# Spacing the transposes of finished attention heads behind the last projection slab, and a home in freed buffers for two output weights

## The chip, the cores and the metric

The kernel runs on one NeuronCore of a Trainium2 chip. The metric is the device time of one execution in microseconds (us), as the median of several. The core has five engines that run beside each other, each through its own list of instructions in order: TensorE (PE in the profile: matrix products and transposes, with PEld for the loading of its stationary operand), VectorE (DVE), ScalarE (ACT), GpSimd (POOL), and SyncE (SP), whose queue here only starts DMA transfers. PE writes its results to PSUM, a small memory of eight banks; the other operands live in SBUF.

## The reference

The model is a trunk of two layers over 512 tokens of width 1024. The first layer holds a causal convolution module, the second differential attention; each is followed by a gated feed-forward block (SwiGLU) and by a gated per-layer embedding. All is float32. The change touches the end of the second layer's attention. For each of eight heads `h`, with two sets of queries and keys of 64 channels, and values of 128 channels:

```python
qkv = x @ w_qkv                       # x is rms-normed before
q, k = rms_norm(q), rms_norm(k)       # per head and set
logits = q @ k.T + bias, causal       # two sets c = 0, 1
w = softmax(logits[0]) - lam * softmax(logits[1])
o = rms_norm(w @ v) * sub_g * (1 - lambda_init)
h = h + concat(o over heads) @ w_o    # 1024 x 1024
```

Then comes `h = h + swiglu(rms_norm(h))`, and then `h = h + sigmoid(rms_norm(h) @ w_gate) * (p @ w_proj)`, where `p @ w_proj` does not depend on `h`.

## The kernel before

Activations are held transposed: channels on the 128 partitions in eight chunks, tokens along the row. To keep float32 precision, every large product is made of three matmuls (`mm3`, lines 165 to 167): each operand is split into a high part `hi`, rounded to a shorter format, and a remainder `lo`, and the kernel sums lo·hi, hi·lo and hi·hi. So each weight tile of 128 x 1024 takes a load by SP into `wraw` (two buffers, line 154), a cast on ACT into `whi` (line 158) and a subtraction on VectorE into `wlo` (line 160). `whi` and `wlo` are rings of four buffers each; a new weight's cast waits until PE has done with the weight four places before it. Activations are split in the same way by `split_scaled` (lines 179 and 180: ACT, then VectorE).

The order of the instructions on each engine is not the order of the source. The program is built with a planner (`schedule_with_timeline_sim=True`): it plays the program through with its own estimates of durations, lets each engine take the earliest instruction in source order that is ready by that estimate, and writes the order down. The chip then runs each engine's list in that fixed order, with semaphore waits. Buffers of a tag go to the next tile of that tag when all readers of an earlier one are done.

The attention is made of 32 blocks, eight heads by four blocks of 128 queries. Each passes four stages:

- `stage_s` (line 953): scores on PE into an `sc` bank (two banks), bias and row extreme on VectorE (line 972), exponential on ACT (976), the combination of both sets on VectorE (979 to 981).
- `stage_t` (984): transposes on PE into a `tp` bank (two banks, line 989), evacuated by ACT (991).
- `stage_a` (997): product with the values on PE (1003) into the head's `mm` bank (four banks), evacuated by ACT (1008). With the fourth block of a head come its norm factors (1011 to 1020) and the scaling on POOL (1022).
- `stage_o` (1026), once per head: four transposes on PE into a `tp` bank (1029), then the split by ACT and VectorE (179, 180) into the tiles `A0` to `A15`, which are the operands of the output product.

The list `stages` (1037 to 1041) holds the first three stages in a software pipeline: block count `n` runs from 0 to 34, and a count issues the scores of block `n`, the transposes of block `n - 2` and the value product of block `n - 3`. While the projection slabs of queries, keys and values are multiplied (1047 to 1061), 63 of these 96 stages are issued between their matmuls. Behind the last slab 33 are left, from `n` = 22 on, and `step()` (1066) issues them one at a time: three steps beside each of the eight feature projections `p @ w_proj` (`project`, 1077 to 1083, two products each; their two weights are called projection weights below), and then one step after each product of the output projection (`linear`, called in 1095, with `heads_until` ahead of each product so that its head is there). After its stage, `step()` looks whether heads are finished: a head counts as finished when `(n - LA - 3) // 4` exceeds its number, with `LA = 3`; when no stages are left, `n` is set to 99.

`linear` (571) makes eight output chunks `m` of eight products `k` each (`k` is the head). Chunks 0 and 1 are made together, the others one by one. Each takes a weight from the ring and sums in an `mm` bank. `add_attn` (1091) adds a chunk to `h` and prepares the norm and operands of the feed-forward block. Behind it, lines 1096 to 1103 copy the first four feature projections to other tiles by DMA, and the feed-forward block begins; its first operands are normed into tiles of the tags C2, C3, C4 and split into C0, C1 and C5 (lines 618 to 625).

The tags C0 to C5 (two buffers each) hold the queries and keys of a pair of heads during the attention: C0 and C1 the queries, C2 to C5 the keys and their remainders. Two pairs are there at a time.

Of the kernel before, what the change touches and what calls it, by code (L numbers as in the profile page):

```python
# [13 lines left out]
F32R = mybir.dt.float32r  # L14
# [6 lines left out]
P = 128  # L21
S = 512
D = 1024
NC = D // P
NH = 8
# [49 lines left out]
LA = 3  # L75
# [17 lines left out]
def trunk(ctx, tc, xT, pT, wts, diag, dww, vec, rel, onehot, lamv, out):  # L93
    nc = tc.nc
    V, A, G, T = nc.vector, nc.scalar, nc.gpsimd, nc.tensor
# [7 lines left out]
    def sb(shape, tag, bufs, dt=F32):  # L103
        uid[0] += 1
        return pool.tile(shape, dt, tag=tag, name=f"{tag}_{uid[0]}", bufs=bufs)

    def ps(tag, bufs, shape=(P, S)):
        uid[0] += 1
        return psum.tile(list(shape), F32, tag=tag, name=f"{tag}_{uid[0]}", bufs=bufs)

    mm = lambda: ps("mm", 4)
    sc = lambda: ps("sc", 2)
# [20 lines left out]
    t = wk()[:, 0:P]  # L133
# [4 lines left out]
    t = tp()  # L138
# [4 lines left out]
    wnext = [0]  # L143
    loaded = [None]

    def weight(n=1024, pieces=1, between=(), eng=V, after=None, behind=None):
        i = wnext[0]
        wnext[0] += 1
        raw = sb([P, 1024], "wraw", 2)
        hi = sb([P, 1024], "whi", 4, F32R)  # L150
        lo = sb([P, 1024], "wlo", 4, F32R)
        for k in range(pieces):
            cut = slice(k * n // pieces, (k + 1) * n // pieces)
            loaded[0] = nc.sync.dma_start(raw[:, cut], wts[i, :, cut])
            if k < len(between):
                between[k]()
            with tc.issue_after(behind.ins) if behind else nullcontext():
                A.copy(hi[:, cut], raw[:, cut])  # L158
            with tc.issue_after(after.ins) if after else nullcontext():
                eng.tensor_tensor(lo[:, cut], raw[:, cut], f(hi[:, cut]), ALU.subtract)  # L160
        return hi, lo

    def mm3(acc, a, b, first, last):
        (ah, al), (bh, bl) = a, b
        T.matmul(acc, al, bh, start=first, stop=False)  # L165
        T.matmul(acc, ah, bl, start=False, stop=False)  # L166
        return T.matmul(acc, ah, bh, start=False, stop=last)  # L167

    def wpart(w, k):
        return tuple(t[:, k * P : (k + 1) * P] for t in w)  # L170
# [71 lines left out]
    def load(c):  # L242
        return lambda: nc.sync.dma_start(h[c], xT[c])

    w0 = weight(pieces=2, between=(load(0),))
    norm.operands(0)
    w1 = weight(pieces=2, between=(load(1), load(2)))
    pair_loads = [loaded[0]]
    pairs = [(w1, w0)]
# [4 lines left out]
    for c in range(1, NC):  # L254
        norm.operands(c)
    pairs.append((weight(), weight())[::-1])
    pair_loads.append(loaded[0])
    for c in range(NC):
# [19 lines left out]
    def project(ph, m, w, o, step=lambda: None):  # L278

        acc = mm()  # L280
        for k in range(2):
            last_product[0] = mm3(acc, wpart(w, 2 * (m % 4) + k), ph[k], k == 0, k == 1)
            step()
        A.copy(o, acc)
        return o
# [4 lines left out]
    accs = {}  # L290
# [275 lines left out]
            if c >= 1:  # L566
                z_lo.append(V.tensor_tensor(z[c - 1][1], y[c - 1], f(z[c - 1][0]), ALU.subtract))

    def linear(n_in, src, consume, group0=1, before=None, after=None, first=(None,) * 3, then=(None, None)):


        m = 0
        while m < NC:
            g = group0 if m == 0 else 1
            if m == group0:
                ws = [weight(n_in * P, behind=then[0], after=then[1])]
            else:
                ws = [weight(n_in * P, after=first[i] if m == 0 else None) for i in range(g)]
            accs = [mm() for _ in range(g)]
            for k in range(n_in):  # L580
                if before:
                    before(k)
                for w_, a_ in zip(ws, accs):
                    mm3(a_, wpart(w_, k), src[k], k == 0, k == n_in - 1)
                    if after:
                        after()
            for i in range(g):
                consume(m + i, accs[i])
            m += g
# [3 lines left out]
    def add_conv(m, acc):  # L593
        V.scalar_tensor_tensor(h[m], acc, col("b_pw2", m), h[m], ALU.add, ALU.add)
        norm.chunk(m)

    linear(NC, z, add_conv, 3, first=(None, last_sum[0], shifted), then=(z_hi[5], z_lo[5]))


    def ffn(norm, after, space):  # L600
# [133 lines left out]
        for at, (f0, n) in enumerate(PARTS):  # L734
            hid = []
            for pair in range(n // 2):
# [3 lines left out]
                if (at, pair) in SEVEN:  # L740
                    while making:
                        feed()
                    i = wnext[0]
                    wnext[0] += 4
                    gs = strassen(i)
                    for t in gs:
                        A.activation(t, t, AF.Silu)
                    us = strassen(i + 1)
                    for o, (t, g) in enumerate(zip(us, gs)):
                        V.tensor_tensor(t, t, g, ALU.mult)  # L750
                        first, step = (H2, H2) if o else (0, S + H2)
                        hs, ls = (bass.AP(x.tensor, x.offset + first, [list(x.ap[0]), [step, 2], [1, H2]]) for x in (hi, lo))
                        A.copy(hs, t.rearrange("p (a s) -> p a s", a=2))
                        V.tensor_tensor(ls, t.rearrange("p (a s) -> p a s", a=2), f(hs), ALU.subtract)
                    continue
# [30 lines left out]
            def add(m, acc):  # L786
                V.tensor_tensor(h[m], acc, h[m], ALU.add)  # L787
                if at == len(PARTS) - 1:
                    after.chunk(m)

            linear(n, hid, add, 2)

    def ple(norm, pp, after, last_cuts=1):
# [41 lines left out]
    for k in range(2):  # L835
        t = tp()
# [27 lines left out]
    def slab(n, cols):  # L864
        per = 1024 // cols
        ws = [weight(eng=G if i < n else V) for i in range(NC // per)]
        return [tuple(t[:, j * cols : (j + 1) * cols] for t in w) for w in ws for j in range(per)]
# [156 lines left out]
    ot = {}  # L1024

    def stage_o(hd):
        t = tp()
        for i in range(4):
            T.transpose(t[:, i * P : (i + 1) * P], osb[hd][:, i * P : (i + 1) * P], ident)
        hi = sb([P, S], f"A{2 * hd}", 1, F32R)  # L1030
        lo = sb([P, S], f"A{2 * hd + 1}", 1, F32R)
        split_scaled(t, gains[:, 1:2], hi, lo)
        ot[hd] = (hi, lo)
# [9 lines left out]
    def take(n):  # L1043
        got, stages[:n] = [s for _, s in stages[:n]], []
        return got

    waiting = None
    for what, at, pace in QKV:
        ws = slab(GLO if what == "q" and at > 0 else 0, P * at[1] if what == "v" else S)
        for tb in range(4):  # L1050
            if (what, at, tb) == ("v", (6, 2), 0):
                ph = pfeatures(1, [both(sb([P, 2, S], t, 1, F32R)) for t in ("B0", "B1")])
            between = take(3 * pace[tb])
# [7 lines left out]
                waiting = unit(at, ws, tb, between)  # L1061


    done = [0]

    def step():
        if stages:
            n, s = stages.pop(0)
            s()
        else:  # L1070
            n = 99
        while done[0] < NH and (n - LA - 3) // 4 > done[0]:
            stage_o(done[0])
            done[0] += 1

    pp = []
    for m in range(NC):
        if m % 4 == 0:
            w = weight()
        step()  # L1080
        if m % 2 == 0:
            o2 = sb([P, 2, S], f"B{m // 2 + 2}", 1) if m < 4 else sb([P, 2, S], f"C{m // 2 + 1}", 2)
        pp.append(project(ph, m, w, o2[:, m % 2], step))
# [7 lines left out]
    def add_attn(m, acc):  # L1091
        V.tensor_tensor(h[m], acc, h[m], ALU.add)
        norm.chunk(m)

    linear(NC, ot, add_attn, 2, heads_until, step)
    for m in (0, 1):
        o = sb([P, S], f"D{m + 2}", 1)
        nc.sync.dma_start(o, pp[m])
# [140 lines left out]
```

## Time and profile before

| | us |
|---|---|
| median of three runs (lowest to highest) | 1248.58 (1246.25 to 1249.45) |
| the profiled execution, whole | 1246.33 |
| its span, first to last instruction | 1244.6 |
| PE busy | 1232.6 (99%) |
| VectorE busy | 879.7 (71%) |
| ScalarE busy | 613.9 (49%) |
| GpSimd busy | 266.3 (21%) |

The granted clock of PE is 0.997 over the span. Times in the views count from the start of the span. A row of the timeline has the start, the length, the engine, the line of the kernel, the operation, the tiles written and read, shapes, and a count; a bracket at its end is the idle time of the engine before it and the work that ended it. In views of waits stand the total, the times and the longest. Matmuls overlap: on PE the distance from start to start is the cost, and not the length. The last slab's products end at 763.4 us, and the last product of the output projection stands near 844 us.

### The profile page before, as it was taken

Reading aid. Unit: us, or ns where it says so; the run is one execution under the profiler, and the core shown is the slowest. Engines: PE = TensorE matmul, PEld = TensorE weight load, DVE = VectorE, ACT = ScalarE, POOL = GpSimd, SP = SyncE. Lnnn points to the kernel's source line nnn. Section 1 sums busy time; section 2 is a strip of 40 time slices with the busy share of each in tenths; the row PEclk is TensorE's granted clock in tenths of the full one; section 3 lists DMA queues with packets and bytes.
Section 4 is the critical chain, followed back from the end, with each engine's and each line's share of the span. In section 5 each row is a group of like instructions: output and inputs, shape, how many; then the busy total and the mean of one; then the engine's idle time right before and its main releaser. Section 6 shows DMA issues by size and latency. Waiting matters only on the chain.

```text
span 1244.6 us, 18577 instructions
## 1 busy us (share of the span) xinstructions
PE 1232.6 (99%) x7170; PEld 1086.2 (87%) x7170; DVE 879.7 (71%) x1417; ACT 613.9 (49%) x1019; POOL 266.3 (21%) x232
## 2 busy tenths in 40 slices
PE   9999999999999999999999999999999999999998
PEld 7888788898999899988888988878898999899887
DVE  6998856965598558667667879547965597458665
ACT  6743555442355235446567778536442355235441
POOL 2852621000000000042516543131000000000130
PEclk9999999999999999999999999999999999999999
DMA  7666232654467444243232224132663577353241
GB/s 284 214 190 193 73 102 85 174 139 132 111 182 180 139 108 121 68 148 97 83 100 77 77 60 157 48 98 72 187 159 112 128 174 189 120 123 107 76 136 68
DMA packets 60597, 158.39 MB, mean 127 GB/s; under 512 B 6451, under 2 KB 11059, under 8 KB 60508
## 3 DMA queue, kind: packets, MB, share of 16 engines
q1 hardware_dynamic: 53776, 136.99, 34.8%
q0 software_dynamic: 4608, 16.78, 8.2%
q10 hardware_dynamic: 2124, 3.43, 0.9%
q8 instruction: 56, 0.92, 0.3%
q14 instruction: 33, 0.27, 0.1%
HBM read 151.91 MB, written 4.21 MB: 125 GB/s over the span
## 4 chain that ended last, share of the span: by engine, by line
PE 95%; DVE 3%; issue 1%; ACT 1%; DMA 0%; SPq 0%; DVEq 0%; ACTq 0%
PE mm L165 26%; PE mm L166 25%; PE mm L167 25%; PE tp L167 2%; PE tp L166 2%; PE tp L165 2%; PE sc L362 2%; PE sc L166 1%; PE sc L167 1%; PE sc L165 1%; PE mm L1003 1%; PE tp L989 1%; PE mm L362 1%; DVE wlo L160 1%; PE sc L970 1%
## 5 line engine op out<-in xcount | busy, mean ns | idle before, releaser
L165 PE MATMUL mm<-A,wlo 128*128 128x512 f32 (+1 forms) x904 | 307.2, 345 | 3.7 <-ACT A L179 2.0
L167 PE MATMUL mm<-A,whi 128*128 128x512 f32 (+1 forms) x904 | 309.8, 343 | 0.0
L166 PE MATMUL mm<-A,whi 128*128 128x512 f32 (+1 forms) x904 | 309.2, 343 | 0.0
L158 ACT CAST whi<-wraw 128x1024 fp32r<-128x1024 f32 (+2 forms) x150 | 151.1, 1014 | 218.9 <-PE mm L167 99.8
L160 DVE TENSOR_TENSOR wlo<-wraw,whi 128x1024 fp32r<-128x1024 f32 (+2 forms) x147 | 185.2, 1262 | 61.7 <-ACT whi L158 61.3
L165 PEld LDWEIGHTS mm<-A,wlo 128*128 128x128 f32 x904 | 171.4, 190 | 24.7 <-ACT A L179 2.6
L166 PEld LDWEIGHTS mm<-A,whi 128*128 128x128 f32 x904 | 171.4, 190 | 20.0 <-DVE A L180 0.8
L167 PEld LDWEIGHTS mm<-A,whi 128*128 128x128 f32 x904 | 171.4, 190 | 19.6 <-issue 0.2
L167 PE MATMUL mm<-B,whi 128*128 128x512 f32 x368 | 143.3, 390 | 0.0
L166 PE MATMUL mm<-B,whi 128*128 128x512 f32 x368 | 143.3, 390 | 0.0
L165 PE MATMUL mm<-B,wlo 128*128 128x512 f32 x368 | 141.3, 392 | 0.0
L676 POOL DMA_DIRECT2D C<-in_wts x32 | 28.1, 878 | 511.3 <-DVE h L787 180.1
L205 POOL TENSOR_TENSOR acc<-acc,wk 128x512 f32<-128x512 f32 x35 | 56.9, 1626 | 217.7 <-ACT wk L204 109.6
L167 PEld LDWEIGHTS mm<-B,whi 128*128 128x128 f32 x368 | 69.1, 188 | 14.9
L166 PEld LDWEIGHTS mm<-B,whi 128*128 128x128 f32 x368 | 69.2, 188 | 14.2
L165 PEld LDWEIGHTS mm<-B,wlo 128*128 128x128 f32 x368 | 69.1, 188 | 14.2
L165 PE MATMUL mm<-whi,A 128*128 128x512 f32 (+1 forms) x224 | 81.5, 366 | 0.0
L166 PE MATMUL mm<-wlo,A 128*128 128x512 f32 (+1 forms) x224 | 81.4, 365 | 0.0
L167 PE MATMUL mm<-whi,A 128*128 128x512 f32 (+1 forms) x224 | 81.1, 364 | 0.0
L787 DVE TENSOR_TENSOR h<-mm,h 128x512 f32<-128x512 f32 x48 | 33.0, 688 | 64.5 <-PE mm L167 64.4
L230 POOL TENSOR_TENSOR r<-v,mhalf 128x8 f32<-128x8 f32 (+1 forms) x30 | 44.9, 1498 | 94.6 <-DVE v L228 87.5
L669 DVE TENSOR_TENSOR wlo<-wraw,whi 128x1024 fp32r<-128x1024 f32 x32 | 39.2, 1225 | 33.4 <-ACT whi L668 33.3
(263 smaller groups left out, 2615.6 us busy)
## 6 DMA issues: line engine op xcount, KB each, us to landing
wraw<-in_wts SPq DMA_DIRECT2D x162, 512.0 KB, 3.7
C<-in_wts SPq DMA_DIRECT2D x32, 512.0 KB, 4.4
C<-in_wts POOLq DMA_DIRECT2D x32, 512.0 KB, 5.8
bias<-in_wts SPq DMA_DIRECT2D x32, 256.0 KB, 3.4
wraw<-in_wts SPq DMA_DIRECT2D x16, 384.0 KB, 3.1
D<-in_diag SPq DMA_DIRECT2D x22, 256.0 KB, 4.8
C<-in_diag SPq DMA_DIRECT2D x16, 256.0 KB, 5.2
h<-in_xT SPq DMA_DIRECT2D x8, 256.0 KB, 5.1
```

Of the source, the lines that this page charges most:

```text
L158: A.copy(hi[:, cut], raw[:, cut])
L160: eng.tensor_tensor(lo[:, cut], raw[:, cut], f(hi[:, cut]), ALU.subtract)
L165: T.matmul(acc, al, bh, start=first, stop=False)
L166: T.matmul(acc, ah, bl, start=False, stop=False)
L167: return T.matmul(acc, ah, bh, start=False, stop=last)
L205: self.last = self.eng.tensor_tensor(self.acc, self.acc, sq, ALU.add)
L230: last_pow[0] = G.tensor_tensor(r[:, :n], v[:, :n], mhalf[:, :n], ALU.pow)
L362: last_tap[0] = T.matmul(acc[:, g * P : (g + 1) * P], w, ups[c][:, g, LEAD - m : LEAD - m + P], start=(m == 0), stop=(m == LAGS - 1),)
L669: V.tensor_tensor(lo, raw, f(hi), ALU.subtract)
L676: nc.gpsimd.dma_start(q, wts[i + 2].rearrange("p (a s) -> p a s", a=2), accum_op=ALU.add)
L787: V.tensor_tensor(h[m], acc, h[m], ALU.add)
L970: T.matmul(acc[:, :n], qs[c][:, i, cut], kl[c][:, i, 0:n], start=False, stop=True)
```

## The change

Two edits. In `step()`, a `while` becomes an `if`: at most one finished head is transposed in a step, and, as long as stages are left, only in every third step. And `linear` gets an argument `homes`: for output chunks 4 and 5 (the fifth and sixth weight), `hi` and `lo` go to buffers of C0 and C1, and of C2 and C5, in place of the ring, and their sums are made in `sc` banks in place of `mm` banks.

```diff
-    def weight(n=1024, pieces=1, between=(), eng=V, after=None, behind=None):
+    def weight(n=1024, pieces=1, between=(), eng=V, after=None, behind=None, home=None):
         i = wnext[0]
         wnext[0] += 1
         raw = sb([P, 1024], "wraw", 2)
-        hi = sb([P, 1024], "whi", 4, F32R)
-        lo = sb([P, 1024], "wlo", 4, F32R)
+        if home:
+            hi, lo = (sb([P, 2, S], t, 2, F32R).rearrange("p a s -> p (a s)") for t in home)
+        else:
+            hi, lo = (sb([P, 1024], t, 4, F32R) for t in ("whi", "wlo"))
...
-    def linear(n_in, src, consume, group0=1, before=None, after=None, first=(None,) * 3, then=(None, None)):
+    def linear(n_in, src, consume, group0=1, before=None, after=None, first=(None,) * 3, then=(None, None), homes={}):
...
-                ws = [weight(n_in * P, after=first[i] if m == 0 else None) for i in range(g)]
-            accs = [mm() for _ in range(g)]
+                ws = [weight(n_in * P, after=first[i] if m == 0 else None, home=homes.get(m)) for i in range(g)]
+            accs = [sc() if m in homes else mm() for _ in range(g)]
...
-    done = [0]
+    done, steps = [0], [0]
 
     def step():
+        steps[0] += 1
         if stages:
             n, s = stages.pop(0)
             s()
         else:
             n = 99
-        while done[0] < NH and (n - LA - 3) // 4 > done[0]:
+        if done[0] < NH and (n - LA - 3) // 4 > done[0] and (n == 99 or steps[0] % 3 == 0):
             stage_o(done[0])
             done[0] += 1
...
-    linear(NC, ot, add_attn, 2, heads_until, step)
+    linear(NC, ot, add_attn, 2, heads_until, step, homes={4: ("C0", "C1"), 5: ("C2", "C5")})
```

## The prediction

> **What bounds the kernel now.** I read the page's first part, then the list of what TensorE (PE) waited for over the whole run, then the stretch after the last projection slab, engine by engine.
>
> ```profile
> span 1244.6 us, 18577 instructions
> PE 1232.6 (99%) x7170; PEld 1086.2 (87%) x7170; DVE 879.7 (71%) x1417; ACT 613.9 (49%) x1019; POOL 266.3 (21%) x232
> ```
>
> ```profile
> PE mm L165 <- ACT A L179: 2.0, 2, 1.2
> PE mm L165 <- DVE wlo L160: 1.8, 1, 1.8
> PE tp L140 <- POOL ident masks.py:199: 1.5, 1, 1.5
> PE sc L969 <- DVE st L972: 1.5, 3, 1.0
> PE tp L989 <- DVE A L180: 0.3, 1, 0.3
> ```
>
> PE is the bound: 1232.6 of 1244.6 us. The waits (total, times, longest) are few, and the change doesn't alter what PE computes, so it can win only waits and slow clock. Three of the five rows lie in its stretch in whole (L160, L969, L989) and the first in part. Windows of that stretch show both (columns: window, length, then busy time of PE, its weight loads, DVE, ACT, POOL, then granted clock, DMA share, GB/s):
>
> ```profile
> 763.50:781.00 17.50, 15.60 (x85) 12.66 (x84) 16.97 (x48) 15.47 (x39) 3.40 (x4) 0.90 0.56 183
> 773.00:777.40 4.40, 2.77 (x13) 1.37 (x11) 4.30 (x13) 4.40 (x11) 0.00 (x0) 1.00 0.71 225
> 777.40:780.90 3.50, 3.35 (x16) 3.12 (x17) 3.25 (x12) 2.43 (x8) 0.00 (x0) 0.51 0.52 190
> 783.30:817.00 33.70, 33.70 (x185) 28.77 (x184) 12.85 (x41) 14.11 (x32) 6.56 (x6) 1.00 0.09 24
> ```
>
> From 763.5 to 781 VectorE (DVE) is full, 16.97 of 17.5 us: there DVE sets the pace, not PE. PE runs dry from 773 to 777.4 (2.77 of 4.40 busy), and then its clock is granted at 0.51 for 3.5 us. From 783.3 to 817 PE has no gap, while DVE and ACT are under half busy. PE's own rows name the dry places; a bracket is idle time and its releaser:
>
> ```profile
> 772.43 0.60 PE L1029 MATMUL tp<-ident,D 128*128 128x128 f32 x4
> 773.31 0.63 PE L1029 MATMUL tp<-ident,D 128*128 128x128 f32 x4
> 774.27 0.47 PE L969 MATMUL sc<-C,C 128*128 128x512 f32 x1 [0.33 <-DVE st L972]
> 775.14 0.47 PE L969 MATMUL sc<-C,C 128*128 128x512 f32 x1 [0.17 <-DVE st L972]
> 776.80 0.33 PE L969 MATMUL sc<-C,C 128*128 128x128 f32 x1 [0.96 <-DVE st L972]
> 777.55 1.75 PE L989 MATMUL tp<-ident,big 128*128 128x128 f32 x7 [0.32 <-DVE A L180]
> ...
> 783.26 0.47 PE L165 MATMUL mm<-B,wlo 128*128 128x512 f32 x1
> ```
>
> The four brackets sum to 1.78 us. The L1029 rows are finished heads being transposed (`stage_o`). The last row is the fifth feature projection: its products stood unused through the dry places. On DVE in the same microseconds:
>
> ```profile
> 772.42 0.74 DVE L180 SCALAR_TENSOR_TENSOR A<-tp,lam,A 128x512 fp32r<-128x512 f32 x1
> ...
> 774.91 1.22 DVE L160 TENSOR_TENSOR wlo<-wraw,whi 128x1024 fp32r<-128x1024 f32 x1
> 776.05 0.68 DVE L972 CUSTOM_DVE_ANT_0 rb<-sc,bias 128x512 f32<-128x512 f32 x1
> 776.66 1.41 DVE L180 SCALAR_TENSOR_TENSOR A<-tp,lam,A 128x512 fp32r<-128x512 f32 x2
> ```
>
> Every L180 here belongs to a transposed head; each holds DVE some 0.7 us in front of an L972, which alone frees the `sc` bank PE waits for. The second dry place is at the head that finishes last:
>
> ```profile
> 807.46 1.06 PE L1003 MATMUL mm<-B,wth 128*128 128x128 f32 x8
> ...
> 816.58 0.60 PE L1029 MATMUL tp<-ident,D 128*128 128x128 f32 x4
> 817.95 1.20 PE L165 MATMUL mm<-A,wlo 128*128 128x512 f32 x4 [0.78 <-ACT A L179]
> ...
> 820.35 0.39 PE L166 MATMUL mm<-A,whi 128*128 128x512 f32 x1
> 820.58 0.39 PE L167 MATMUL mm<-A,whi 128*128 128x512 f32 x1
> 822.72 0.50 PE L165 MATMUL mm<-A,wlo 128*128 128x512 f32 x1 [1.75 <-DVE wlo L160]
> ```
>
> At 807.46 the last attention block is multiplied, at 816.58 its head is transposed; between them PE ran what it had of output weights 1 to 4. Nothing was left to cover the two splits (0.78), and then the fifth weight wasn't ready (1.75). Why not, ACT and DVE say:
>
> ```profile
> 791.77 1.05 ACT L158 CAST whi<-wraw 128x1024 fp32r<-128x1024 f32 x1
> ...
> 819.64 2.00 ACT L158 CAST whi<-wraw 128x1024 fp32r<-128x1024 f32 x2 [1.75 <-PE mm L167]
> ```
>
> ```profile
> 821.45 1.22 DVE L160 TENSOR_TENSOR wlo<-wraw,whi 128x1024 fp32r<-128x1024 f32 x1
> ```
>
> The casts of weights 5 and 6 waited for PE to release a ring buffer, though their raw data had been asked for at 776.16 and 794.11, with 3.6 us to landing:
>
> ```profile
> 776.16 0.33 SPq L154 DMA_DIRECT2D wraw<-in_wts  x1
> 794.11 0.33 SPq L154 DMA_DIRECT2D wraw<-in_wts  x1
> ```
>
> ```profile
> DMA to landing us min/median/max: 3.5/3.6/4.6
> ```
>
> **The change, part by part.** *Pacing.* Before, the first block step (block count n=22) meets the condition for heads 0 to 3 at once, and all four transposes are issued there. After, counting steps by the code: heads 0 to 3 at steps 3, 6, 9, 12, head 4 at 15 (was 11), head 5 at 24 (was 23), heads 6 and 7 at 33 and 34 as before. No instruction is added. Each moved head is four transposes, one ACT split and one L180. Of the three L180 quoted, I take it that those ahead of the waits go behind them. The waits of 0.33 and 0.17 are each shorter than one L180 (1.41 for two less 0.74 for one: 0.67) and vanish; the 0.96 still stands behind the L160 of 774.91 (the third output weight, which stays) and loses 0.67, leaving 0.3; the 0.32 waits for an L180 itself and vanishes. Gain 1.78 - 0.3 = 1.5 us. Bounds: 1.78 above; below, a loss of 1.2, if nothing fills the places of the two transposes at 772.43 and 773.31 (0.60 and 0.63). I take 1.5, because six products of the fifth projection (783.26) are free to move there.
>
> *The clock.* 3.35 us of PE work ran at 0.51: at full clock it is 3.35 x 0.51 = 1.7, a gain of 1.65. Bounds: 1.65 above; a second such stretch, minus 1.65, below. I take 1.65, since the slow stretch starts where the waits end. [...]
>
> *Weights 5 and 6 in freed buffers.* C0, C1, C2, C5 hold pairs of query/key operands; one of two buffers of each is free once head 5's last scores are multiplied (775.14 and its partner). Weight 5's data land at 776.16 + 3.6 = 779.8; its cast (1.05) and L160 (1.22) end near 782.5; then its raw buffer takes weight 6, ready some 6 us later, or near 800 if it has to follow the buffer of 794.11. Both precede 807. The four instructions move from 819.64 into the window 783.3 to 817, where ACT has 33.7 - 14.1 = 19.6 us idle and DVE 20.9: price nothing under that cover, and 2.3 us per weight on DVE and ACT if they fall into the full 763.5 to 781. The `sc` banks for their sums are free after the last scores, before 797. So PE gets 14 more products of three matmuls, 0.23 us apart (820.35 and 820.58), 0.69 us a product, 9.7 us that need no last head. The 0.78 vanishes behind two of them (bounds 0 to 0.78). The 1.75 vanishes (bounds 0 to 1.75): weights 5 and 6 are there, and weights 7 and 8, whose casts now wait for the ring instead, need 822.67 - 819.64 = 3.0 us from release, under some 12 remaining products, 8 us.
>
> The copies of projections 2 and 3 into C2 (L1102) now wait for the other C2 buffer, until the last scores near 796, and can hold the SP queue only where they stand ahead of a load. The next reader of these buffers is far off:
>
> ```profile
> 773.70 0.52 SPq L1102 DMA_DIRECT2D C<-B  x1
> ```
>
> ```profile
> 864.77 3.22 ACT L624 CAST C<-C 128x512 fp32r<-128x512 f32 x6
> ```
>
> That leaves 60 us; price nothing. Weights 5 and 6 give C0, C1, C2 and C5 back by about 840 as well.
>
> *Sum.* 1.5 + 1.65 + 0.78 + 1.75 = 5.7 us. The profiled execution took 1246.33 (span 1244.6 and 1.7 around it): 1240.6 against itself. The median of the runs shown is 1248.58, 2.25 above that execution: 1242.9 against it. I forecast the median, **1243**.
>
> **Rivals.**
> 1. *DVE still sets the pace behind the slab.* For it: 16.97 of 17.5 us, and only some L180 leave. The order on each engine is fixed by a planner's estimates, which put nothing into the gaps before. Then only 0.78 + 1.75 = 2.5 come: 1246.
> 2. *The waits go, the slow clock stays* or comes elsewhere: 5.7 - 1.65 = 4.0: 1244.6. [...] Against: clock and waits adjoin in the rows.
> 3. *The change doesn't do what it says.* The planner doesn't place the new splits before 807, or PE meets other waits of the same size: 1248.6. Against: 20 us of room on both engines.
> 4. *Slower: a cast that holds ACT.* `wraw` has two buffers, and one is held by the fourth output weight until its cast at 791.77. Weights 5 and 6 must pass through the other in turn, with 3.6 us per load, while softmax exponentials and evacuations stand behind the cast on ACT. The planner does place casts before their data:
>
> ```profile
> 874.83 1.05 ACT L158 CAST whi<-wraw 128x1024 fp32r<-128x1024 f32 x1 [3.71 <-DMA wraw<-in_wts]
> ```
>
> Two such waits among the attention blocks are 7.4 us; with one more slow-clock stretch, less the 2.5 won: 7.4 + 1.65 - 2.5 = 6.5 longer, 1255. It decides from about 1 us of such wait per cast that PE sees. Against: from 783.3 on PE has 33.7 us without a gap, so there is slack. [...]
>
> **How the numbers follow.** Forecast 0.37; rival 1 0.24; rival 2 0.12; rival 3 0.12; rival 4 0.10; 0.05 unnamed. About 0.3%, 3.7 us, is what a measurement of this kernel can tell from no change. Faster by more: 0.35 from the forecast, 0.07 from rival 2, 0.06 from rival 1 and unnamed: 0.48. Slower: 0.12 (rival 4 and a little of 3). Same: 0.40. The range runs from 1240, the sum against the profiled execution with its upper bounds, to 1249, no gain; rival 4 lies outside. The likeliest alone: 1240.6 to 1244.
>
> **What would show it.** In the changed profile: L1029 groups no longer adjacent behind 767; no clock of 0.5 near 777; the PE rows L969 <- L972 gone or under 0.5 us; no wait on L160 near 822; two L158 casts more between 776 and 807; the last head's products follow its transposes without a bracket. I am wrong if PE's waits there still sum to over 2 us, if ACT rows show a cast waiting for `in_wts` between 776 and 807 with PE brackets behind, or if a new slow-clock stretch stands there.

## The result, and the profile after

The changed kernel takes 1241.19 us (median of five executions, 1239.75 to 1242.65) against 1248.38 us before (five, 1246.25 to 1249.45). The ratio is 0.9949 with a 95% interval of 0.9938 to 0.996: 6.4 us less, between 5.0 and 7.7. (The two medians alone differ by 7.2 us; that too lies in the interval.) The profiled execution took 1239.75 us, its span is 1238.0 us, 6.6 less than before. In the changed kernel the line numbers from 150 on are two or three higher: L165 to L167 are now L167 to L169, L160 is L162, L180 is L182, L972 is L974, L1003 is L1005, L1029 is L1031.

First the head of the profile's page, and what TensorE (PE) waited for over the whole run (total, times, longest):

```profile
span 1238.0 us, 18578 instructions
PE 1230.4 (99%) x7170; PEld 1084.6 (88%) x7170; DVE 879.3 (71%) x1417; ACT 613.2 (50%) x1019; POOL 268.0 (22%) x232
```

```profile
PE tp L140 <- POOL ident masks.py:199: 1.5, 1, 1.5
PE mm L167 <- DVE wlo L162: 0.6, 1, 0.6
PE mm L167 <- ACT A L181: 0.5, 1, 0.5
```

The waits on score banks are gone, the wait on a weight's remainder fell from 1.8 to 0.6 us, and of the waits on ACT only the one at the start of the kernel is left. The same windows as in the prediction (window, length, busy time of PE, its weight loads, DVE, ACT, POOL, then granted clock, DMA share, GB/s):

```profile
773.00:777.40 4.40, 4.40 (x32) 3.71 (x31) 4.35 (x13) 4.40 (x12) 0.00 (x0) 1.00 0.19 47
777.40:780.90 3.50, 3.50 (x18) 2.87 (x17) 3.43 (x12) 3.50 (x9) 0.00 (x0) 1.00 0.67 240
783.30:817.00 33.70, 33.70 (x186) 28.70 (x186) 14.51 (x41) 13.07 (x30) 5.50 (x6) 1.00 0.26 79
```

PE is full and its clock is whole. DVE is at least as full as before in the first two (4.35 of 4.40 against 4.30, 3.43 of 3.50 against 3.25). So the place is still one where DVE works without a pause, but PE no longer stands behind it. PE's own rows say why:

```profile
772.00 0.60 PE L991 MATMUL tp<-ident,big 128*128 128x128 f32 x4
772.43 0.83 PE L1005 MATMUL mm<-B,wtl 128*128 128x128 f32 x6
...
773.45 0.60 PE L1031 MATMUL tp<-ident,D 128*128 128x128 f32 x4
773.80 0.48 PE L971 MATMUL sc<-C,C 128*128 128x512 f32 x1
...
775.03 1.06 PE L1005 MATMUL mm<-B,wth 128*128 128x128 f32 x8
776.02 0.33 PE L971 MATMUL sc<-C,C 128*128 128x128 f32 x1
...
776.90 0.48 PE L167 MATMUL mm<-B,wlo 128*128 128x512 f32 x1
```

Of the two bunched heads (772.43 and 773.31 before) one still stands near its place (773.45); the next follows only at 776.29. Around them the attention's own next stages have moved up: the value products of head 5's third block stand at 772.43 and those of its fourth at 775.03, where before they came at 779.09 and 781.65. The fifth projection moved from 783.26 to 776.90. On DVE one head's L182 less stands ahead of these score rows, and two heads' L182 (776.49 and 778.53) follow them:

```profile
774.13 1.22 DVE L162 TENSOR_TENSOR wlo<-wraw,whi 128x1024 fp32r<-128x1024 f32 x1
775.27 0.69 DVE L974 CUSTOM_DVE_ANT_0 big<-sc,bias 128x512 f32<-128x512 f32 x1
...
775.88 0.69 DVE L974 CUSTOM_DVE_ANT_0 rb<-sc,bias 128x512 f32<-128x512 f32 x1
...
776.49 0.75 DVE L182 SCALAR_TENSOR_TENSOR A<-tp,lam,A 128x512 fp32r<-128x512 f32 x1
```

The weight's L162 at 774.13 still stands ahead of both score rows, as the prediction said of the L160 before; PE now has the value products of 775.03 to do in that time.

At the last head:

```profile
816.69 0.60 PE L1031 MATMUL tp<-ident,D 128*128 128x128 f32 x4
...
818.06 0.39 PE L168 MATMUL sc<-A,C 128*128 128x512 f32 x1
...
822.16 1.07 PE L167 MATMUL mm<-A,wlo 128*128 128x512 f32 x4
...
826.01 0.39 PE L169 MATMUL sc<-A,C 128*128 128x512 f32 x1
827.02 0.50 PE L167 MATMUL mm<-A,wlo 128*128 128x512 f32 x1 [0.62 <-DVE wlo L162]
```

The last products of weight 4 that need no last head and the products with C (weights 5 and 6 in their homes) cover the split of the last head, and no bracket stands at 818. The products of weights 1 to 4 with the last head come only at 822.16. ACT:

```profile
779.19 1.06 ACT L160 CAST C<-wraw 128x1024 fp32r<-128x1024 f32 x1
...
786.83 1.05 ACT L160 CAST C<-wraw 128x1024 fp32r<-128x1024 f32 x1 [1.00 <-DMA wraw<-in_wts]
...
823.95 2.00 ACT L160 CAST whi<-wraw 128x1024 fp32r<-128x1024 f32 x2 [5.94 <-PE mm L169]
```

The casts of weights 5 and 6 moved up from 819.64; the second waited 1.00 us for its data, and PE has no bracket behind it. Weights 7 and 8 now wait for the ring, until 823.95.

### The profile page after: what moved, and what is told of

The parts are those of the page before. It is cut to its first block, busy times and chain, and to the rows that moved or that the text cites. A ratio compares the mean times of both kernels' runs of the same rounds, so it can differ in the third digit from the quotient of the medians.

```text
span 1238.0 us, 18578 instructions
## 1 busy us (share of the span) xinstructions
PE 1230.4 (99%) x7170; PEld 1084.6 (88%) x7170; DVE 879.3 (71%) x1417; ACT 613.2 (50%) x1019; POOL 268.0 (22%) x232
## 3 DMA queue, kind: packets, MB, share of 16 engines
q10 hardware_dynamic: 2124, 3.43, 0.9%
## 4 chain that ended last, share of the span: by engine, by line
PE 97%; DVE 2%; ACT 1%; issue 0%; DMA 0%; SPq 0%; DVEq 0%
PE mm L167 26%; PE mm L168 25%; PE mm L169 25%; PE tp L169 2%; PE tp L168 2%; PE tp L167 2%; PE sc L364 2%; PE sc L167 2%; PE sc L169 1%; PE sc L168 1%; PE mm L1005 1%; PE sc L972 1%; PE sc L971 1%; PE mm L364 1%; PE tp L991 1%; PE mm L320 1%
## 5 line engine op out<-in xcount | busy, mean ns | idle before, releaser
L169 PE MATMUL mm<-A,whi 128*128 128x512 f32 (+1 forms) x888 | 304.1, 343 | 0.0
L168 PE MATMUL mm<-A,whi 128*128 128x512 f32 (+1 forms) x888 | 303.8, 343 | 0.0
L167 PE MATMUL mm<-A,wlo 128*128 128x512 f32 (+1 forms) x888 | 300.2, 343 | 1.1 <-DVE wlo L162 0.6
L160 ACT CAST whi<-wraw 128x1024 fp32r<-128x1024 f32 (+2 forms) x148 | 149.3, 1015 | 219.5 <-PE mm L169 108.6
L162 DVE TENSOR_TENSOR wlo<-wraw,whi 128x1024 fp32r<-128x1024 f32 (+2 forms) x145 | 182.1, 1258 | 59.6 <-ACT whi L160 59.2
L167 PEld LDWEIGHTS mm<-A,wlo 128*128 128x128 f32 x888 | 168.4, 190 | 21.5 <-ACT A L181 1.2
L168 PEld LDWEIGHTS mm<-A,whi 128*128 128x128 f32 x888 | 168.5, 190 | 19.2 <-DVE A L182 0.8
L169 PEld LDWEIGHTS mm<-A,whi 128*128 128x128 f32 x888 | 168.6, 190 | 18.8 <-issue 0.2
L169 PE MATMUL mm<-B,whi 128*128 128x512 f32 x368 | 143.3, 390 | 0.0
L167 PE MATMUL mm<-B,wlo 128*128 128x512 f32 x368 | 141.3, 392 | 0.0
L169 PEld LDWEIGHTS mm<-B,whi 128*128 128x128 f32 x368 | 69.1, 188 | 15.0
L167 PEld LDWEIGHTS mm<-B,wlo 128*128 128x128 f32 x368 | 69.1, 188 | 14.2
L167 PE MATMUL mm<-whi,A 128*128 128x512 f32 (+1 forms) x224 | 81.5, 366 | 0.0
L169 PE MATMUL mm<-whi,A 128*128 128x512 f32 (+1 forms) x224 | 81.1, 364 | 0.0
```

## The experiments

The theory after the result: the two edits work at two separate places and add up. The rivals: one of them brings the whole, by rearranging everything; DVE sets the pace anyway; the half clock belongs to the transposes themselves.

**The spacing alone.** The homes are left out:

```diff
-    linear(NC, ot, add_attn, 2, heads_until, step, homes={4: ("C0", "C1"), 5: ("C2", "C5")})
+    linear(NC, ot, add_attn, 2, heads_until, step)
```

> Only the spacing of the transposed heads; the fifth and sixth output weight go through the ring as before. My theory (the two edits work at two places and add up): the waits on L969-type score rows and the half-clock stretch near 777 us are gone, 1.78 + 1.65 = 3.4 us less; the waits of 0.78 and 1.75 us behind the last head stay. About 3.4 us under the kernel before, ratio 0.9973. Rival (VectorE sets the pace behind the slab, and only work that the homes set free fills PE): the waits near 774 to 778 stay and the time is within 1 us of before, ratio 0.999 to 1.001.

Measured: 1243.25 us against 1248.01, ratio 0.9965 (0.9953 to 0.9977). The two windows and the two rows with a bracket behind the last head:

```profile
773.00:777.40 4.40, 4.40 (x33) 3.72 (x32) 4.34 (x13) 4.40 (x12) 0.00 (x0) 1.00 0.42 113
777.40:780.90 3.50, 3.50 (x18) 2.90 (x17) 3.43 (x11) 3.11 (x8) 0.00 (x0) 1.00 0.72 260
```

```profile
813.56 1.20 PE L167 MATMUL mm<-A,wlo 128*128 128x512 f32 x4 [0.78 <-ACT A L181]
818.33 0.50 PE L167 MATMUL mm<-A,wlo 128*128 128x512 f32 x1 [1.73 <-DVE wlo L162]
```

The first dry place and its half clock are gone, the second stands as before. The rival that DVE sets the pace by its amount of work falls: DVE is as full (4.34 of 4.40), and PE does not wait. The planner changed the order on DVE and on PE together, and no run separates the two. The gain, 4.4 us (2.9 to 5.9 by the interval), holds the expected 3.4, though nearer its lower end.

**The homes alone.** The `while` of `step()` is back:

```diff
-        if done[0] < NH and (n - LA - 3) // 4 > done[0] and (n == 99 or steps[0] % 3 == 0):
+        while done[0] < NH and (n - LA - 3) // 4 > done[0]:
```

> Only the homes of the fifth and sixth output weight; four heads transposed at the first step as before. My theory: the waits of 1.78 us near 774 to 778 and the half-clock stretch behind them stay; 0.78 and 1.1 of the 1.75 us behind the last head go: about 1.9 us less, ratio 0.9985. Rival: the homes alone bring the whole gain of some 6 us, since earlier splits rearrange the order of all engines: ratio 0.995, and no half-clock stretch.

Measured: 1246.22 us against 1248.01, ratio 0.9983 (0.9975 to 0.9992). PE's waits from 763 to 850 us, then rows of PE, a window with PE's busy time and clock, and a row of ACT:

```profile
PE sc L971 <- DVE st L974: 1.5, 3, 1.0
PE tp L991 <- ACT wth L993: 0.6, 1, 0.6
PE mm L167 <- DVE wlo L162: 0.4, 1, 0.4
PE tp L991 <- DVE A L182: 0.3, 1, 0.3
```

```profile
779.50:783.00 3.50, 3.28 (x16) 0.54 0.55 181
```

```profile
784.26 0.33 PE L991 MATMUL tp<-ident,big 128*128 128x128 f32 x1 [0.57 <-ACT wth L993]
```

```profile
781.97 1.05 ACT L160 CAST C<-wraw 128x1024 fp32r<-128x1024 f32 x1 [0.86 <-DMA wraw<-in_wts]
```

The waits on score banks and the half clock are there as before; the homes took most of the second place. A new wait shows: the cast of weight 5 waits 0.86 us for its data ahead of an evacuation, and PE stands 0.57 us for that. So the two edits add, as far as the times can tell: 1 - 0.9965 and 1 - 0.9983 make 0.0052, and both together measure 0.0051 and, in the repeat below, 0.0046, each to within some 0.001.

**One head in every step.** The limit of one per step stays, the third step goes:

```diff
-        if done[0] < NH and (n - LA - 3) // 4 > done[0] and (n == 99 or steps[0] % 3 == 0):
+        if done[0] < NH and (n - LA - 3) // 4 > done[0]:
```

> As the changed kernel, but a finished head may be transposed in every step, not only in every third: at most one per step stays. My theory: heads 0 to 3 come within four steps, so their four splits on VectorE again stand among the scores of head 5 and the first of head 6, and part of the 1.78 us of waits returns, perhaps with the half clock: 1 to 3.4 us more than the changed kernel, ratio 0.996 to 0.998. Rival (only the burst of four in one step hurts): as the changed kernel, ratio 0.995.

Measured: 1246.75 us against 1247.48, ratio 0.9991 (0.9982 to 1.0), scattering from 1243.79 to 1248.64. It is the expected direction but more than expected: by the times nearly all of the gain is lost. The profile below is of the fastest of the ten executions. PE's waits from 773 to 785 us, and the row behind the longest on PE and on ACT:

```profile
PE tp L991 <- ACT wtl L993: 1.6, 1, 1.6
PE sc L971 <- DVE st L974: 0.9, 3, 0.4
PE tp L1031 <- DVE A L182: 0.4, 1, 0.4
PE tp L991 <- DVE st L981: 0.3, 1, 0.3
```

```profile
783.27 0.44 PE L991 MATMUL tp<-ident,big 128*128 128x128 f32 x2 [1.58 <-ACT wtl L993]
```

```profile
781.04 1.05 ACT L160 CAST C<-wraw 128x1024 fp32r<-128x1024 f32 x1 [1.18 <-DMA wraw<-in_wts]
```

Four waits sum to 3.2 us, more than the 1.78 of the kernel before. The longest is rival 4 of the prediction at work: weight 5's cast waits 1.18 us for its data, with evacuations and exponentials queued behind it on ACT, and PE stands 1.58 us. So the limit of one per step is not enough; of the paces, only every step and every third were run. And the homes came without cost in the runs with the third step alone. One head in every step without the homes was not run, so how much of the loss is the heads' alone is not shown.

These waits explain only a part of the lost time: in the two profiled executions this stretch keeps 2.7 us of the gain (table below). What takes the rest in the others is not shown. Of the ten, the four with a mean granted clock of 0.996 or 0.997 took 1247.39 to 1248.64 us, the six with 0.998 to 1.0 took 1243.79 to 1246.93. Where their clock was low is not known.

**Sums in `mm` banks.** The homes stay, the `sc` banks go:

```diff
-            accs = [sc() if m in homes else mm() for _ in range(g)]
+            accs = [mm() for _ in range(g)]
```

> As the changed kernel, but the sums of the fifth and sixth output chunk are made in mm banks, not in sc banks. My theory: the four mm banks are held by chunks 0 to 3 until the last head is there, so no product of chunks 4 and 5 can run before it: the wait of about 0.8 us for the last head's split comes back, while weights 5 and 6 are split early, so that behind it PE waits less than 1.75 us. About 0.8 us more than the changed kernel, 5 less than before: ratio 0.996. Rival (the banks do not matter, the early splits do): as the changed kernel, no wait for the last head, ratio 0.995.

Measured: 1241.23 us, ratio 0.9946 (0.9933 to 0.996), as the changed kernel. PE's rows at the last head:

```profile
814.18 0.60 PE L1031 MATMUL tp<-ident,D 128*128 128x128 f32 x4
815.56 1.20 PE L167 MATMUL mm<-A,wlo 128*128 128x512 f32 x4 [0.78 <-ACT A L181]
```

The wait of 0.78 us is back, as expected; but it is the only one from 763 to 850, for now all of chunks 4 and 5 is left to cover the seventh weight's split. One wait was exchanged for another of 0.62 us, and the time doesn't tell them apart. So for the time the early split is what counts in the homes, and not the banks.

**A third home.** The seventh weight goes to the other buffers of C0 and C1, its sum to an `mm` bank:

```diff
-    linear(NC, ot, add_attn, 2, heads_until, step, homes={4: ("C0", "C1"), 5: ("C2", "C5")})
+    linear(NC, ot, add_attn, 2, heads_until, step, homes={4: ("C0", "C1"), 5: ("C2", "C5"), 6: ("C0", "C1")})
...
-            accs = [sc() if m in homes else mm() for _ in range(g)]
+            accs = [sc() if m in homes and m < 6 else mm() for _ in range(g)]
```

> As the changed kernel, and the seventh output weight too gets a home in the other buffers of C0 and C1, free after the last scores; its sum in an mm bank. My theory: the wait of 0.62 us for the seventh weight's split is gone, 0.6 us less than the changed kernel, ratio to before 0.9944. Rival (its split competes with others on ACT and VectorE, or its raw load comes late): no change or up to 1 us more.

Measured: 1239.78 us, ratio 0.9939 (0.9925 to 0.9952), and PE has no wait from 763 to 850 us. By these numbers it would be better than the changed kernel, so both ran again beside each other:

> The changed kernel once more, on the same chip as the next run and the kernel before. Theory: about 1241.2, ratio to before 0.995, one wait of 0.6 us for the seventh weight's split and none besides in the stretch.

> The kernel with a third home (seventh weight in the other buffers of C0 and C1) once more, beside the changed kernel. Theory: 0.6 us or some more under the changed kernel, 1239.8 to 1240.6; no wait in the stretch. Rival (the earlier difference was scatter): within 0.3 us of the changed kernel.

Measured beside each other: the changed kernel 1241.02 us, ratio 0.9954 (0.9941 to 0.9968); the third home 1241.11, ratio 0.9955 (0.9943 to 0.9967). The wait is gone from the trace again, and the time is not less: 0.6 us lie below the scatter of these runs. The times show no gain.

**The stretch alone.** The scatter can be kept out. Every one of these traces has 7170 products and transposes of PE, and the 4200th (near 741 us) and the 5200th (near 921 to 928 us) stand on the same line with the same shape in each. The time from the one's start to the other's, in one or two profiled executions:

| kernel | us |
|---|---|
| before | 186.56, 186.26 |
| spacing alone | 182.37 |
| homes alone | 185.03 |
| one head in every step, with homes | 183.69, 183.78 |
| sums in `mm` banks | 180.24 |
| changed | 180.34, 180.27 |
| third home | 179.52, 179.39 |

Two executions of one kernel agree within 0.3 us here. Spacing alone is worth 4.0 us, the homes alone 1.4, both 6.1. The 0.7 us by which the sum falls short is about the 0.57 us that PE stands behind the cast of weight 5 in the run of the homes alone, a wait that the changed kernel doesn't have. And the third home is 0.75 to 0.95 us shorter in both of its traces. So the gain is there in the stretch, and what comes before it can hide it: in the repeat PE reached the 1500th product at 294.42 us with the third home and at 290.92 in the changed kernel, long ahead of the change.

**What lowers the clock.** Behind the output projection of the changed kernel, transposes without use are added, and in a control as much time of ordinary products:

```diff
+    t = tp()
+    for i in range(80):
+        j = i % 4
+        T.transpose(t[:, j * P : (j + 1) * P], h[7][:, j * P : (j + 1) * P], ident)
```

> The changed kernel with 80 extra transposes of 128x128 behind the output projection, made from its last chunk into a tp bank and not used: 80 x 0.1 = 8 us of PE work without a wait. Theory A (the half clock of the kernel before came from PE standing idle): the clock stays at 1.0 through them, each takes 0.10 to 0.11 us, the time is about 8 us more than the changed kernel. Theory B (transposes count little as work for whatever grants the clock, so bunched transposes lowered it): the granted clock falls to about 0.5 within or right behind them, each takes 0.2 us, 10 to 16 us more.

> As the run with extra transposes, but 40 ordinary float32 products of 128x128 with the same operands in their place, two passes each, 80 x 0.1 = 8 us. Both theories: the clock stays at 1.0; about 8 us more than the changed kernel. It is the control for the transposes.

Measured: 1249.02 us with the transposes and 1250.89 with the products, one execution each. (The 1.9 us between them come from the start, where the control's clock fell: its 1500th product starts 1.75 us later.) PE's row of the transposes and its windows over them (busy time, clock):

```profile
844.45 8.89 PE L1102 MATMUL tp<-ident,h 128*128 128x128 f32 x80
```

```profile
844.40:848.40 4.00, 4.00 (x38) 1.00 0.44 127
848.40:853.30 4.90, 4.90 (x47) 1.00 0.01 5
```

The next row of PE starts at 853.10, so 80 transposes took 8.65 us, 0.108 each, at full clock to the end; the 40 products (two passes each, 80 rows) took 8.84 us, at full clock too. Transposes without a gap did not lower the clock. That leaves the standing idle; whether it always does, two more profiled executions were to show:

> The kernel before, one more look at its clock. Theory (the clock is set by how much PE does within windows that run on their own, so the same waits lower it in some executions and not in others): the same waits of 1.5 + 0.3 us near 774 to 778; the half-clock stretch may be missing, shorter or elsewhere behind them. Rival (the waits always lower it): granted clock of 0.5 from about 777.4 to 780.9 again.

> The kernel with at most one transposed head in every step, one more look. Its first profile had 3.2 us of waits in the stretch and a full clock at 1243.8 us, while its other executions took up to 1248.6. Theory (free-running windows): the same waits, and in this look a half-clock stretch of some 3.5 us or more is likely behind them, with 2 to 4 us more time. Rival (the scatter has another source): full clock again, and the additional time stands elsewhere.

The kernel before, once more (1245.74 us), with PE's busy time and clock:

```profile
773.00:776.00 3.00, 2.05 (x9) 1.00 0.78 303
776.00:777.00 1.00, 0.49 (x2) 0.83 0.12 33
777.00:779.00 2.00, 1.83 (x9) 0.50 0.86 246
779.00:780.50 1.50, 1.50 (x12) 0.64 0.34 74
```

The same waits, the same half clock, beginning near 776.7 and not at 777.4. With the run of the homes alone the clock fell behind these waits, to 0.5, in three profiled executions of three. The kernel with one head in every step took 1245.75 us in its second profiled execution, with 3.2 us of waits again and a clock of 1.00 in every window from 763 to 840, as in its first. So the expectation for it missed: more idle time, twice, and no half clock.

The traces' records of the clock say more. In the thirteen traces it fell eight times ahead of the kernel's end: three times here, five times in the first 15 us. Seven of these stretches last 3.41 us and one 6.83, twice that; and within a trace all changes lie a whole number of 3.41 us apart (226 times that from the first record to 777.48 in the kernel before). So here the clock changed on a grid of 3.41 us, which lies differently over the rows in each execution. What did PE do in the grid's windows? Here is the kernel before, with the score rows that the prediction leaves out; together with 774.27, 775.14 and 776.80 they are all that starts between 774.07 and 777.48, and no transpose is among them:

```profile
774.58 0.40 PE L970 MATMUL sc<-C,C 128*128 128x512 f32 x1
775.45 0.39 PE L970 MATMUL sc<-C,C 128*128 128x512 f32 x1
776.97 0.27 PE L970 MATMUL sc<-C,C 128*128 128x128 f32 x1
```

Counted by the distance to the next row where PE doesn't wait (0.227 us for 512 columns, 0.175 for 384, 0.12 for 256, 0.11 for 128), that is 4 x 0.227 + 2 x 0.11 = 1.13 us of work. The emptiest window at full clock from 763 to 840 us, estimated in the same way from each execution's rows:

| execution | window (us) | work of PE (us) | clock in the next window |
|---|---|---|---|
| before | 774.07 to 777.48 | 1.13 | 0.5 |
| before, again | 773.24 to 776.66 | 1.24 | 0.5 |
| homes alone | 775.92 to 779.33 | 1.14 | 0.5 |
| one head in every step | 775.15 to 778.56 | 2.01 | 1.0 |
| the same, again | 777.05 to 780.46 | about 2.0 | 1.0 |
| spacing alone | 815.50 to 818.91 | 1.37 | 1.0 |

The value for the second profile of one head in every step is an estimate from the rows of the first, put 1.9 us later: so they give PE's busy time in the four windows of the second from 773.00 to 786.00 us within 0.1 us.

What goes with a fall in these traces is neither the sum of the waits nor the longest one, but how little PE did in one such window; the 3.2 us of waits spread over several, and the window of the spacing alone holds the whole wait of 1.73 us and still more work. In the first 15 us PE's busy time goes the same way: from 4 to 8 us it was 2.54 us in the repeat of the third home and 2.80 in that of one head in every step, behind which the clock fell, and 2.93 to 3.48 us in five executions where it stayed at 1.00. By the count it stayed up there behind windows with some 1.3 us of work (the changed kernel, 4.24 to 7.65) and 1.7 (the kernel before, 2.66 to 6.07). Where the limit lies these windows don't show, and the count knows nothing of what kind the work is. How the grid lies decides little for the kernel with one head in every step: in whatever position, its emptiest window holds 1.51 us or more by the rows from 773 to 785 us of its first profile, where that of the kernel before holds 1.01 to 1.43 us (estimates by the same count). What took the time in the slower of the ten executions is not shown.

## Why the prediction was right

The time lies in the range, and below the forecast of 1243 by 1.8 us. The places and the kind of gain were right; that the sum came so near is in part luck, since two terms were too small and one too large. Of the 1.8 us, 0.9 is the profiled execution (6.6 us less, 5.7 forecast) and 0.8 the distance of the median from it (1.44 us and not 2.25), which is scatter. By its steps:

- *What bounds the kernel*: PE's waits and its clock, at two places. Shown by the two parts run alone. That DVE sets the pace there was too strong: from 773 to 781 it is as full after the change, and PE doesn't wait.
- *Spacing*, forecast 1.5 us: all four brackets, 1.78, went. The step said that the fifth projection's products would fill the places of the transposes. It was rather head 5's own next stages that moved up (772.43 and 775.03), and the projection filled behind them from 776.90. They also covered the 0.3 us that was to remain behind the split of the third weight.
- *The clock*, forecast 1.65: the window has 1.00 where it had 0.51. The rival by which the slow clock stays fell. The step went only by the waits and the slow stretch standing side by side; the table of windows shows what joins them.
- *Last head's split*, forecast 0.78: gone. It is the sums in `sc` banks that did it, for with `mm` banks the 0.78 came back.
- *Seventh weight*, forecast 1.75: only 1.13 went, 0.62 stays. The step that failed is the cover of "some 12 remaining products": they exist, but the planner put most of them (818.06 to 822.16) ahead of the products that release the ring, so that at the release (823.95) less was left than the 3.0 us that the split needs.
- *The sum*: 5.7 forecast; the stretch from the 4200th to the 5200th product gave 6.2 between the two traces that the prediction and the result show (186.56 - 180.34). The brackets add to 1.78 + 0.78 + 1.13 and the clock to 1.65: 5.3. The rest is a mis-sized term: the prediction took brackets for the cost of waits. A matmul's row is longer than the distance to the next one (0.39 against 0.23 for 512 columns), so a bracket begins too late. From start to start, the wait before 775.14 costs 775.14 - 774.58 - 0.23 = 0.33 and not 0.17. Taken so, the four waits of the first place cost 2.45 us in place of 1.78, and the 0.78 costs 0.94: together 0.83 more, which closes the sum. By the same count the spacing alone is worth 2.45 + 1.65 = 4.1; the stretch showed 4.0.
- *Moved copies*: the two copies of projections 2 and 3 went from 771.25 and 773.70 to 789.58 and 790.1, and no instruction waited for them. The step overlooked the copies of projections 0 and 1 (L1098, now L1101). The second one now waits 4.8 us in SP's queue for a head's transposes (L1031), and the load of weight 6 stands behind it: it starts at 783.01, 1.0 us after the end of weight 5's split (782.01), when its buffer was free. The cast of weight 6 then waits 1.00 us for these data, and PE does not. So the price was nothing, though copies did hold SP's queue ahead of a load.
- *Rival 4*, the cast that holds ACT: its wait is there (1.00 us at 786.83) but reaches PE only in the runs with the heads closer together (0.57 and 1.58 us).

## What to carry to other kernels

When a program's order is fixed ahead by estimates, a burst of optional work (here finished heads, transposed from 767.5 on and first multiplied at 791.1 in the kernel before) belongs between the steps of the critical chain, at a measured pace; source order is the tool for it. A wait for a ring's buffer at the end of a phase can be taken away with buffers that have just become free, but the cast that moves up takes its DMA wait along (0.86 to 1.18 us here), in front of all that stands behind it in its engine's order. Cost a wait on TensorE from start to start, not by the bracket (the four waits of the first place: 2.45 us and not 1.78). And where short waits crowd, look at the clock behind them: here waits of 2.45 us brought 1.65 us of slow clock with them.

## What was not expected of the hardware

- The granted clock fell to 0.5 for 3.41 us behind waits of at most 1.0 us each (1.13 to 1.24 us of work in the 3.41 us before the fall; the kernel before, twice, and the homes alone), and not behind a single wait of 1.75 us (the kernel before), nor behind 3.2 us of waits within 9 us (one head in every step, twice).
- 80 float32 transposes ran for 8.65 us, more than two of the grid's windows, at a clock of 1.00, as the products of the control did for 8.84 us. Theory B of that run, by which bunched transposes lower the clock, is not borne out.
- The clock also falls at the start of the kernel, in five of the thirteen profiles, whatever the version, and is a part of the scatter of 2 to 4 us between executions of one kernel: PE's 1500th product starts at 291.46 to 294.42 us in these five, and at 290.13 to 290.92 in the other eight. In the repeat of the third home (1243.11 us in that execution) and of the changed kernel (1241.02), PE's busy time and clock:

```profile
8.00:12.00 4.00, 3.23 (x8) 0.52 1.05 401
```

```profile
8.00:12.00 4.00, 3.36 (x14) 1.00 1.07 406
```
